# Longer slots for split activations: a distance in SBUF that differs from slot to slot

## The chip, the cores and the metric

The kernel runs on one core of a Trainium2 chip. The metric is the device time of one execution in microseconds. Engines are named as in the profile: PE is TensorE, PEld its loading of weights, DVE VectorE, ACT ScalarE, SP SyncE.

## The reference

A decoder trunk of two layers on one sequence of 256 tokens with 2048 features. The first layer is recurrent, the second attends within a window and has attention sinks; each is followed by a SwiGLU feed-forward block of width 5632, and one pair of keys and values is projected between them.

```python
for layer in range(DEPTH):                       # DEPTH = 2
    if layer < N_REC:                            # N_REC = 1
        x = recurrent_block(x, norm1_g[layer], lru_w_in[i], ...)   # 2048 -> 2 x 2048, gates 8 x 256 x 256, out 2048 -> 2048
    else:
        if layer == N_REC:
            k_band, v_band = shared_kv(x, kv_norm_g, w_kv, k_norm_g)   # 2048 -> 2 x 256
        x = attn_block(x, norm1_g[layer], w_q[j], ...)                 # 2048 -> 2048, window 128, out 2048 -> 2048
    x = swiglu_ffn(x, norm2_g[layer], ffn_w_in[layer], ffn_w_out[layer])   # 2048 -> 2 x 5632 -> 2048
```

All of it is float32.

## The kernel before

Activations lie with features on the 128 partitions and the 256 tokens along the free dimension. Each float32 operand of a big product is split into two float32r parts, a high part (the rounded value) and a low part (what the rounding left), and a product is the sum of three matmuls: high weights by high activations, high weights by low activations, and low weights by high activations.

The weights come from HBM in tiles of 128 x 1024 (512 KB), one per *job*. A job is two tiles of the contraction (`k` = 0, 1) by four tiles of 128 output features (`f` = 0 to 3), so 24 matmuls of 128 x 128 weights and 256 columns. `load` (L241) brings a tile into one of four buffers `raw`; `split` writes its high part to one of four buffers `hi` on ACT (L259) and its low part to one of four `lo` on DVE (L260). `stream` goes through the jobs in order: it loads four jobs ahead, splits three jobs ahead, and runs the job's matmuls.

The activations lie in *slots*, 58 of them, which `slot` hands out and `free` takes back in a queue. A slot has 2 x 256 float32 on each partition: the high part in its first half (1024 bytes), the low part in the second. `split_act` fills it (ACT by L113, DVE by L122). Slots also serve as plain float32 scratch. A job needs two slots, `x2[0]` and `x2[1]`, one for each `k`.

`products` writes the matmuls of a job: the weights are a slice of 128 columns (512 bytes) of `hi` or `lo`, and the moving operand is the high half ("a"), the low half ("b") or, in a few places, the whole slot ("h", 512 columns in one matmul) of `x2[k]`:

```python
w = (hi if high else lo)[:, k * 512 + f * P:k * 512 + f * P + P]
args = (ps[f][0][:, 0:c1 - c0], w, x2[k][:, c0:c1])
```

They are at L323, and at L321 where another matmul was put ahead of one. In most jobs the order alternates between `k` = 0 and 1 after two to four matmuls; in the last job of a group it does after three. The gates of the recurrent block have their own matmuls (L641) with slots moving, 24 for each of eight jobs. The projection of keys and values (eight jobs) does twelve matmuls with slots moving (L832) and then twelve with the slots as weights and `hi` or `lo` moving (L841 to L843). Norms, attention scores, transposes and the like are plain float32 matmuls through `pe_other` (L331, L334). `warm` (L268) runs 15 matmuls on zeros at the start.

The buffers are placed one after another in SBUF, in the order in which they are made: parameters, constants, `x`, `raw`, `hi`, `lo`, scratch, and then the slots. On each partition `hi` begins at byte 54752 and each of `hi` and `lo` is 4096 bytes long, so all eight begin at 480 modulo 512. `s0` begins at byte 104992, which is 32 modulo 512, and a slot is 2048 bytes.

Of the kernel before, what the change touches and what calls it, by code (L numbers as in the profile page):

```python
# [17 lines left out]
P = 128  # L18
D = 2048
T = 256  # L20
# [28 lines left out]
class Trunk:  # L49
# [12 lines left out]
    WARM = 15  # L62
    SYNC = (0, 2, 5)
    RUNS = 3
    DVE_TICK = 640.0
    ACT_TICK = 800.0

# [71 lines left out]

    def slot(self, dt=F32R):  # L140
        i = self.slots.popleft()
        s = self.spool.tile([P, 2 * T], dt, tag=f"s{i}", name=f"s{i}")
        self.held[id(s)] = (i, s)
        return s

# [54 lines left out]
    def run_bg(self):  # L200
        self.dve = min(max(self.dve - self.DVE_TICK, -self.SPARE), self.DEBT)
        self.act = min(max(self.act - self.ACT_TICK, -self.SPARE), self.DEBT)
        while self.dve < self.DVE_TICK and self.act < self.ACT_TICK:
            task = next((t for t in self.bg if t[0] <= self.tick), None)
            if task is None:
                break
            self._step(task)
# [81 lines left out]
    def products(self, todo, st, hi, lo, x2, last, keep=False, paired=False):  # L289
# [7 lines left out]
        while rest:  # L297
# [3 lines left out]
            if self.other is not None:  # L301
                self.runs = self.RUNS
            if not keep and self.runs and rest[0][2] != "h":
# [436 lines left out]
    def kv(self, xs, r, gains):  # L740
# [65 lines left out]
        for c in range(8):  # L806
            def mm(hi, lo, c=c):
                if c == 0:
                    st["ps"] = [self.bank() for _ in range(4)]
                    self.DVE_TICK, self.ACT_TICK, self.SPARE = self.LATER  # L810

# [319 lines left out]
```

## Time and profile before

| | |
|---|---|
| median of three runs | 1990.26 us (1989.77 to 1990.41) |
| span of the profiled execution | 1988.6 us |
| its time beside the median | the span is 1.7 us below the median of the runs; no other time of that execution was taken |
| PE busy | 1982.0 us, 16684 matmul records |
| DVE, ACT busy | 1271.2 us, 1067.9 us |
| HBM read | 371.88 MB, 188 GB/s over the span |

A matmul's duration in the profile reaches from its start to the modelled end of its pipeline, and the next one starts before that. How fast matmuls follow one another is read from their starts: from the timeline, from the chain in order of time, or from a count in a stretch.

### The profile page before, as it was taken

The numbers are of one execution on the slowest core, as the hardware profiler recorded it, in microseconds if no ns is written. First come the engines' busy times: TensorE is split into PE (matmuls) and PEld (weight loads), VectorE is DVE, ScalarE is ACT, GpSimd is POOL, SyncE is SP. The second block draws the span as 40 slices with busy tenths as digits, with TensorE's granted clock in tenths as the row PEclk, the third lists the DMA queues.
The fourth block names the chain that finished last, engine by engine and source line by source line (L and its number), as shares of the span: only waits on it lengthen the run. The fifth ranks groups of instructions, "written<-read, shape, count | busy, mean of one in ns | idle before, by whom it ended". The sixth has DMA issues, their size and how long they took to land.

```text
span 1988.6 us, 40066 instructions
## 1 busy us (share of the span) xinstructions
PE 1982.0 (100%) x16684; PEld 1935.5 (97%) x16684; DVE 1271.2 (64%) x2049; ACT 1067.9 (54%) x1624; POOL 0.2 (0%) x4
## 2 busy tenths in 40 slices
PE   9999999999999999999999999999999999999999
PEld 9999999999999999999999889999999999999999
DVE  8988876556556655545668786755565565554453
ACT  7798655444444444444556775544454454444442
POOL 0000000000000000000000000000000000000000
PEclk9999999999999999999999999999999999999999
DMA  8555655565556555556555435565566656656663
GB/s 279 185 187 182 211 191 192 196 196 191 192 195 196 191 192 196 195 191 194 197 186 167 134 101 163 188 197 195 191 193 196 195 191 194 197 193 203 204 208 128
DMA packets 105302, 376.58 MB, mean 189 GB/s; under 512 B 11808, under 2 KB 14240, under 8 KB 105120
## 3 DMA queue, kind: packets, MB, share of 16 engines
q1 hardware_dynamic: 104832, 373.88, 57.8%
q8 instruction: 130, 2.13, 0.4%
q14 instruction: 52, 0.43, 0.1%
q10 hardware_dynamic: 288, 0.14, 0.0%
HBM read 371.88 MB, written 2.10 MB: 188 GB/s over the span
## 4 chain that ended last, share of the span: by engine, by line
PE 99%; ACT 0%; DVE 0%; DMA 0%; issue 0%; ACTq 0%
PE b L323 94%; PE b L334 2%; PE b L641 1%; PE b L331 1%; PE b L832 1%; ACT s L113 0%; PE b L321 0%; PE b L841 0%; PE b L842 0%; PE b L843 0%; DMA x<-in_x 0%; DVE s L131 0%; DVE lo L260 0%; ACT L113 0%; DVE s L122 0%
## 5 line engine op out<-in xcount | busy, mean ns | idle before, releaser
L323 PE MATMUL b<-s,hi 128*128 128x256 f32 (+1 forms) x10276 | 1431.9, 285 | 0.4 <-ACT s L113 0.4
L323 PEld LDWEIGHTS b<-s,hi 128*128 128x128 f32 x10276 | 1313.4, 188 | 30.4 <-ACT s L113 0.7
L260 DVE TENSOR_TENSOR lo<-raw,hi 128x1024 fp32r<-128x1024 f32 (+1 forms) x705 | 861.4, 1223 | 651.2 <-ACT hi L259 648.1
L259 ACT ACTIVATE hi<-raw 128x1024 fp32r<-128x1024 f32 (+1 forms) x705 | 745.7, 1059 | 817.7 <-PE b L323 756.7
L323 PE MATMUL b<-s,lo 128*128 128x256 f32 x5504 | 831.8, 277 | 0.0
L323 PEld LDWEIGHTS b<-s,lo 128*128 128x128 f32 x5504 | 720.4, 188 | 2.4 <-issue 0.8
L113 ACT ACTIVATE s<-h 128x256 fp32r<-128x256 f32 (+1 forms) x106 | 40.8, 411 | 23.8 <-DVE h L122 23.8
L113 ACT ACTIVATE t<-b 128x256 f32<-128x256 f32 x136 | 49.8, 374 | 2.5 <-PE b L323 0.3
L113 ACT ACTIVATE s<-x,par 128x256 fp32r<-128x256 f32 x80 | 38.6, 499 | 19.3 <-DVE x L122 13.6
L113 ACT ACTIVATE s<-s 128x256 f32<-128x256 f32 (+1 forms) x112 | 39.6, 409 | 5.7 <-DVE s L126 5.5
L113 ACT ACTIVATE h<-h 128x256 f32<-128x256 f32 (+1 forms) x104 | 38.8, 375 | 2.1
L113 ACT ACT_TABLE_LOAD x30 | 38.5, 1283 | 0.5
L126 DVE SCALAR_TENSOR_TENSOR s<-x,par,s 128x256 fp32r<-128x256 f32 x80 | 37.5, 482 | 1.4 <-ACT s L113 0.8
L122 DVE TENSOR_TENSOR h<-b,rstd 128x256 f32<-128x256 f32 x100 | 37.6, 417 | 0.0
L122 DVE TENSOR_TENSOR x<-x,b 128x256 f32<-128x256 f32 x64 | 24.1, 418 | 21.0 <-PE b L323 21.0
L113 ACT ACTIVATE s<-s,h 128x128 f32<-128x128 f32 x64 | 28.3, 443 | 13.3 <-DVE h L131 13.2
L122 DVE TENSOR_TENSOR h<-h,rstd 128x256 f32<-128x256 f32 x94 | 35.4, 419 | 0.0
L122 DVE TENSOR_TENSOR h<-h,h 128x256 f32<-128x256 f32 x88 | 35.0, 420 | 0.4 <-ACT h L113 0.4
L122 DVE TENSOR_TENSOR s<-h,s 128x256 fp32r<-128x256 f32 x88 | 35.2, 420 | 0.1
L122 DVE TENSOR_TENSOR h<-b,t 128x256 f32<-128x256 f32 x92 | 34.6, 417 | 0.0
L122 DVE TENSOR_TENSOR s<-s,s 128x256 fp32r<-128x256 f32 (+1 forms) x80 | 30.9, 422 | 3.5 <-ACT s L113 3.5
L334 PE MATMUL b<-s,s 64*128 64x256 f32 (+3 forms) x292 | 29.0, 302 | 0.1
(99 smaller groups left out, 566.4 us busy)
## 6 DMA issues: line engine op xcount, KB each, us to landing
raw<-in_ffn_in SPq DMA_DIRECT2D x352, 512.0 KB, 3.5
raw<-in_ffn_out SPq DMA_DIRECT2D x176, 512.0 KB, 4.3
raw<-in_lru_in SPq DMA_DIRECT2D x63, 512.0 KB, 3.6
raw<-in_lru_out SPq DMA_DIRECT2D x32, 512.0 KB, 3.7
raw<-in_w_q SPq DMA_DIRECT2D x32, 512.0 KB, 3.3
raw<-in_w_o SPq DMA_DIRECT2D x32, 512.0 KB, 3.3
raw<-in_gate SPq DMA_DIRECT2D x8, 512.0 KB, 3.9
raw<-in_kv SPq DMA_DIRECT2D x8, 512.0 KB, 4.3
```

Source lines behind the costliest of these rows:

```text
L113: self.nc.scalar.activation(out, in_, func, **kw)
L122: self.nc.vector.tensor_tensor(out, a, b, op)
L126: self.nc.vector.scalar_tensor_tensor(out, a, s, b, op0, op1)
L259: self.nc.scalar.activation(hi[:, q], raw[:, q], AF.Copy)
L260: self.nc.vector.tensor_tensor(lo[:, q], raw[:, q], hi[:, q].bitcast(F32), ALU.subtract)
L323: self.nc.tensor.matmul(*args, **kw)
L331: self.other = self.ins(f(*args, **kw))
L334: self.other = self.ins(f(*args, **kw))
L641: nc.tensor.matmul(out[j], (hi if high else lo)[:, c:c + P], x2[kt][:, q:q + T], start=kt == 0 and high > q, stop=kt == 1 and not high)
L832: nc.tensor.matmul(ps[f][:, 0:T], w0, x2[kt][:, q:q + T], start=k0 + kt == 0 and high > q, stop=k0 + kt == ND - 1 and not high)
```

## The change

Each slot's tile gets 8 more float32 (32 bytes) on each partition, and the slot that is handed out is its first 512 elements. Nothing else differs: the line numbers behind it grow by 1 or 2, so L323 becomes L325.

```diff
     RUNS = 3
+    STEP = 8
...
     def slot(self, dt=F32R):
         i = self.slots.popleft()
-        s = self.spool.tile([P, 2 * T], dt, tag=f"s{i}", name=f"s{i}")
+        w = self.spool.tile([P, 2 * T + self.STEP], dt, tag=f"s{i}", name=f"s{i}")
+        s = w[:, 0:2 * T]
         self.held[id(s)] = (i, s)
```

Slot `i` then begins 2080 bytes, not 2048, after the one before it.

## The prediction

> **What bounds the kernel now.** I read the page first: the busy times, the row of the granted clock and the chain that ended last, then the costliest groups.
>
> ```profile
> span 1988.6 us, 40066 instructions
> ...
> PE 1982.0 (100%) x16684; PEld 1935.5 (97%) x16684; DVE 1271.2 (64%) x2049; ACT 1067.9 (54%) x1624; POOL 0.2 (0%) x4
> ...
> PEclk9999999999999999999999999999999999999999
> ...
> PE 99%; ACT 0%; DVE 0%; DMA 0%; issue 0%; ACTq 0%
> PE b L323 94%; PE b L334 2%; PE b L641 1%; PE b L331 1%; PE b L832 1%; ACT s L113 0%; PE b L321 0%; PE b L841 0%; PE b L842 0%; PE b L843 0%; DMA x<-in_x 0%; DVE s L131 0%; DVE lo L260 0%; ACT L113 0%; DVE s L122 0%
> ...
> L323 PE MATMUL b<-s,hi 128*128 128x256 f32 (+1 forms) x10276 | 1431.9, 285 | 0.4 <-ACT s L113 0.4
> L323 PEld LDWEIGHTS b<-s,hi 128*128 128x128 f32 x10276 | 1313.4, 188 | 30.4 <-ACT s L113 0.7
> ```
>
> PE is busy all the span, the clock is granted in full, and 99% of the chain is matmuls on PE that wait for nothing else. So the time is the number of matmuls times the distance in time from one start to the next, which I call the spacing. Only what changes the spacing can move the end. The mean of a matmul (285 ns) is no spacing, since matmuls are pipelined. The load of weights (188 ns) is longer than the spacing too, so the load for the next matmul runs beneath the present one, and the two read SBUF at once: that is what the change touches.
>
> The spacing comes from the chain in order of time, whose pieces give a start, a length and a count of matmuls.
>
> ```profile
> 74.19 2.72 PE b L641 x24
> 76.91 21.76 PE b L323 x192
> ...
> 123.14 5.44 PE b L641 x48
> ...
> 155.81 22.78 PE b L323 x192
> 178.59 5.65 PE b L641 x48
> ```
>
> Here stands the fact on which I build. The same 192 matmuls of the same line take 21.76 us in one piece (113.3 ns each) and 22.78 us in another (118.6 each). The 48 of L641 take 5.44 us (113.3) or 5.65 (117.7). The spacing has two states, about 4.4 ns (4%) apart, in the same kernel, with the clock full. I call them the short and the long state. The piece at 155.81 may hold some waits besides, so I take the smaller step, the 4.4 of L641.
>
> The long stage of feed-forward matmuls is all in the short state. The groups of the stretch from 400 to 1000 us, with shapes kept apart, show it:
>
> ```profile
> L323 PE MATMUL b<-s,hi 128*128 128x256 f32 x3149 | 418.8, 276 | 0.0
> L323 PE MATMUL b<-s,lo 128*128 128x256 f32 x1766 | 263.6, 276 | 0.0
> L323 PE MATMUL b<-s,hi 128*128 128x512 f32 x189 | 53.5, 392 | 0.0
> ```
>
> Counting a 512-column matmul as two units of 256 columns there are 3149 + 1766 + 2 x 189 = 5293 units in 600 us: 113.4 ns. The third row says one thing more. It has one load of weights (188 ns, above) for 512 columns, and its second 256 columns cost 392 - 276 = 116 ns, no less than a unit with a load beneath it. So the 113.3 seem to be the price of streaming 256 columns, and not of a meeting of the two reads.
>
> Elsewhere the long state holds for long. In the stretch from 1171 to 1230 us the groups have a longer mean for the same shape:
>
> ```profile
> L323 PE MATMUL b<-s,hi 128*128 128x256 f32 x220 | 31.3, 282 | 0.0
> L323 PE MATMUL b<-s,lo 128*128 128x256 f32 x120 | 19.0, 280 | 0.0
> ```
>
> **The change, part by part.** It removes and adds no instruction, and in the built programs the order on every engine and every wait are the same. Only addresses move. Before, slot i begins at 104992 + 2048 i bytes, so every slot is 32 modulo 512; the buffers hi and lo begin at 480 modulo 512, and all slices of weights are whole steps of 512 bytes. The distance from weights to moving operand is 64 modulo 512 for every one of the matmuls of L321, L323, L641 and L832. After, a slot is 2080 bytes and the distance is 64 + 32 i modulo 512: sixteen distances, each for three or four of the 58 slots. Counting in the built order, the distance changes at 5000 of 16,193 places, once in 3.2 matmuls.
>
> The groups of the whole run, with shapes kept apart, say how much work that is:
>
> ```profile
> L323 PE MATMUL b<-s,hi 128*128 128x256 f32 x9570 | 1291.3, 277 | 0.4 <-ACT s L113 0.4
> L323 PE MATMUL b<-s,lo 128*128 128x256 f32 x5504 | 831.8, 277 | 0.0
> L323 PE MATMUL b<-s,hi 128*128 128x512 f32 x706 | 201.6, 393 | 0.0
> ...
> L321 PE MATMUL b<-s,hi 128*128 128x512 f32 x13 | 6.6, 510 | 0.0
> ```
>
> That is 9570 + 5504 + 2 x 706 + 2 x 13 = 16,512 units; eight jobs of gates and eight of keys and values, with 24 each, make 16,896.
>
> What other distances cost is shown in one place only, the projection of keys and values. There L832 has slots as moving operand and hi or lo as weights (distance 64), and after each twelve, L841 to L843 have it the other way round (slots as weights, hi or lo moving: distance -64, which is 448); at each turn one matmul runs over a load at distance 0. From the timeline (start, length, engine and line):
>
> ```profile
> 1013.80 0.39 PE L832 MATMUL b<-s,hi 128*128 128x256 f32 x2
> ...
> 1015.16 0.28 PE L841 MATMUL b<-hi,s 128*128 128x256 f32 x1
> ...
> 1016.46 0.28 PE L843 MATMUL b<-hi,s 128*128 128x256 f32 x1
> 1016.58 0.40 PE L832 MATMUL b<-s,hi 128*128 128x256 f32 x2
> 1016.82 0.28 PE L832 MATMUL b<-s,lo 128*128 128x256 f32 x1
> ...
> 1018.00 0.28 PE L841 MATMUL b<-hi,s 128*128 128x256 f32 x1
> ...
> 1019.37 0.39 PE L832 MATMUL b<-s,hi 128*128 128x256 f32 x2
> ```
>
> Twelve of L832 take 1015.16 - 1013.80 = 1.36 us (113.3 ns): short state. At the very matmul where the distance changes the state becomes long: 1016.58 - 1015.16 = 1.42 us (118.3). Back at 64 it stays long (1018.00 - 1016.58 = 1.42), and at the next turn to 448 it falls back to short (1019.37 - 1018.00 = 1.37). No wait and no other work marks the first turn. So the state isn't fixed by the distance, since both occur at 64 and at 448, but a change of distance can throw it over, and it then lasts. The 48 matmuls average (1019.37 - 1013.80) / 48 = 116.0 ns.
>
> This is the nearest row to a kernel whose distance keeps changing, so I take 116.0 as its spacing. Now it is 113.4, and some 130 us of the span (25 us from 156, half of the projection of keys and values, most of 1160 to 1230, some shorter pieces, an estimate by the views above) are at 4.4 more: about 1100 units, 0.3 ns in the mean, so 113.7. The difference is 2.3 ns x 16,896 = 39 us.
>
> To this comes the turn itself. The three starts from 1016.46 to 1016.82 are 360 ns apart, against 3 x 117.7 = 353: some 6 ns for a turn. The turns from 1018.00 on show about 2 or less. With 5000 turns that is between 0 and 30 us, of which 16,896 / 12 x 6 = 8 us at most are in the 116.0 already. A step of 32 is smaller than the 384 here, so I take 6 us. The sum is 1988.6 + 39 + 6 = 2033.6 for the span, and with the 1.7 us between the span and the median of 1990.26 it is 2035 us.
>
> The bounds of this cost: below, every matmul at the short spacing, 0.3 x 16,896 = 5 us less than now, 1985; above, every matmul in the long state, (117.7 - 113.7) x 16,896 = 68 us, and all turns at 6 ns, 22 us more: 2080.
>
> The rest is covered. ScalarE and VectorE write and read the slots at new addresses, but DVE has 36% of the span idle and ACT 46%; even 5% on all DVE work (64 us) would lie beside PE. If that cover were gone, PE would wait for slots, and the idle columns of L323 (0.4 and 0.0 us now) would show it. The transfers go to raw, which doesn't move. The few fp32 matmuls of L331 and L334 read two slots or a slot and a constant; at 3% of the chain (L334 2%, L331 1%: 60 us) even a 4% change is 2 us.
>
> **The rivals.** First: *no change*. If the state hangs on when a matmul starts and not on the addresses, the kernel stays at 1990, 1985 to 1994. For it speaks that both states occur at distance 64. The Trainium skill, "SBUF — State Buffer", section "SBUF: two separate sides", says that PE has two independent read ports, one for the moving operand and one for the weights, and that PE never waits on anyone there; by this rule the change moves nothing and the time is 1990. The trace disagrees in part: the spacing went from 113.3 to 118.3 at the matmul where the operands change places. Also on this side lies the case in which mixed distances end each long stretch early: at best 5 us, 1985.
>
> Second: *faster*. If the 113.3 themselves come from how the slots lie (all of them are 32 modulo 64 now, half of them would be 0 modulo 64), then some distances are below it. No row shows a shorter spacing, so I bound the gain by the only step that rows show, 4.4 ns, for half of the units: 2.2 x 16,896 = 37 us, 1953; for a quarter, 1971. Against it stands the 512-column row: its second half has no load beneath it and costs the same. The Trainium skill, "TensorE: Matmul & The Clock Gate", section "Wait — 56ns, not 53.3ns?", gives N / 2.4 GHz + 2.5 ns at full clock, 109.2 ns for 256 columns. By that figure there would be 4.1 ns to win on each unit; here 113.3 is measured, and no run tells yet why.
>
> Third: *much slower*. If some of the sixteen distances hold the long state or worse whatever came before, and each turn costs its 6 ns, the time goes to the upper bound, 2058 to 2080, and past it if a distance exists that costs more than 118. Nothing in the trace shows more than 118 for long.
>
> That the change doesn't do what it says is ruled out by the addresses in the built program.
>
> **How the numbers follow.** A measurement of this kernel tells some 0.2% (4 us) from no change. A mixture of the two states, 1995 to 2058: 0.54. The upper case, 2058 and more: 0.12. No change: 0.12, of which 0.02 are below 1986. Faster by a lower spacing: 0.22. So faster 0.24, same 0.10, slower 0.66. The forecast is that of the likeliest case, 2035. The range leaves out about one in ten on each side: down to 1968, just past a quarter of the units at the shorter spacing, and up to 2078; alone, the likeliest case would have 1995 to 2058.
>
> **What would show it.** Right: in the profile after, the clock stays full, idle times stay near zero, and the chain's pieces of 192 matmuls of L323 (by its new line number) at 77 us take about 22.3 us instead of 21.76; in the stretch from 400 to 1000 us the mean of a 256-column matmul rises from 276 to about 279, and fewer units fit in it, some 5170 instead of 5293. The projection of keys and values, which alternates already, changes least. Wrong: the mean there falls below 276 (then slot placement was the price), stays at 276 (then the distance doesn't matter), or PE shows idle time before matmuls, named by a releaser.

## The result and the profile after

The changed kernel takes 2060.0 us (2059.58 to 2060.41), the kernel before 1990.3 us: a ratio of 1.0349, interval 1.0335 to 1.0364. It is slower and inside the range; it moved by 69.7 us, half as much again as the 45 that were forecast. The profiled execution spans 2058.2 us, 69.6 us more than before.

The page after, in the rows that answer to those of before:

```profile
span 2058.2 us, 40066 instructions
...
PE 2051.6 (100%) x16684; PEld 2003.9 (97%) x16684; DVE 1272.4 (62%) x2049; ACT 1068.0 (52%) x1624; POOL 0.2 (0%) x4
...
PEclk9999999999999999999999999999999999999999
...
PE 99%; ACT 0%; DVE 0%; DMA 0%; issue 0%; ACTq 0%
...
L325 PE MATMUL b<-s,hi 128*128 128x256 f32 (+1 forms) x10276 | 1477.6, 289 | 0.5 <-ACT s L114 0.5
...
L325 PE MATMUL b<-s,lo 128*128 128x256 f32 x5504 | 856.1, 281 | 0.0
```

The clock is full, PE has the same 16684 records and no more idle time (0.5 us before L325, 0.4 before), and DVE and ACT are busy as long as before (1272.4 and 1068.0 us). The same matmuls simply follow one another more slowly. In the chain in order of time (start, length, line, count) the pieces of equal work in the recurrent block show by how much:

```profile
76.20 2.83 PE b L643 x24
79.03 22.71 PE b L325 x192
...
127.33 5.68 PE b L643 x48
...
161.33 22.76 PE b L325 x192
184.09 5.68 PE b L643 x48
```

192 matmuls took 21.76 us before, and take 22.71 (118.3 ns each). The second 192, which before ran in the long state (22.78), are unchanged at 22.76. The 48 of the gates are all at 5.68, where before some were at 5.44 and some at 5.65. So the short state is nearly gone. The stretch from 400 to 1000 us, groups with shapes kept apart:

```profile
L325 PE MATMUL b<-s,hi 128*128 128x256 f32 x3000 | 416.1, 281 | 0.0
L325 PE MATMUL b<-s,lo 128*128 128x256 f32 x1696 | 262.5, 281 | 0.0
L325 PE MATMUL b<-s,hi 128*128 128x512 f32 x192 | 55.0, 395 | 0.0
```

3000 + 1696 + 2 x 192 = 5080 units in 600 us are 118.1 ns, against 113.4. Worked out from the starts of all 256-column matmuls that follow another without a gap, the mean spacing is 113.6 ns before and 118.1 after; 4.5 ns for some 15,450 of them is 69.5 us, about the whole difference.

### The profile page after: what moved, and what is told of

The parts are those of the page before. It is cut to its first block, busy times and chain, and to the rows that moved or that the text cites. A ratio compares the mean times of both kernels' runs of the same rounds, so it can differ in the third digit from the quotient of the medians.

```text
span 2058.2 us, 40066 instructions
## 1 busy us (share of the span) xinstructions
PE 2051.6 (100%) x16684; PEld 2003.9 (97%) x16684; DVE 1272.4 (62%) x2049; ACT 1068.0 (52%) x1624; POOL 0.2 (0%) x4
## 4 chain that ended last, share of the span: by engine, by line
PE 99%; ACT 0%; DVE 0%; DMA 0%; issue 0%; ACTq 0%
PE b L325 94%; PE b L336 2%; PE b L643 1%; PE b L333 1%; PE b L834 1%; ACT s L114 0%; PE b L323 0%; PE b L843 0%; PE b L845 0%; PE b L844 0%; DMA x<-in_x 0%; DVE s L132 0%; ACT L114 0%; DVE lo L262 0%; DVE s L902 0%
## 5 line engine op out<-in xcount | busy, mean ns | idle before, releaser
L325 PE MATMUL b<-s,hi 128*128 128x256 f32 (+1 forms) x10276 | 1477.6, 289 | 0.5 <-ACT s L114 0.5
L325 PEld LDWEIGHTS b<-s,hi 128*128 128x128 f32 x10276 | 1350.2, 188 | 32.0 <-ACT s L114 0.8
L325 PE MATMUL b<-s,lo 128*128 128x256 f32 x5504 | 856.1, 281 | 0.0
L325 PEld LDWEIGHTS b<-s,lo 128*128 128x128 f32 x5504 | 740.2, 188 | 2.3 <-issue 0.8
```

What stands on the lines that cost most here:

```text
L325: self.nc.tensor.matmul(*args, **kw)
```

## The experiments

Two theories stood against each other. *Change*, which the forecast used: both states occur at any distance, and it is the changing that throws the matmuls into the long one. *Set*: the spacing belongs to the distance, and most of the sixteen are worse than 64. All runs but the last two leave the slots as they were before the change or move them as a whole; in every kernel the matmuls and their order are those of before. Distances are the moving operand's address less that of the weights loaded beneath it, which are the next matmul's. The runs `a_blocks`, `b_perjob`, `c_align`, `h_sixteen` and `d_fine` were timed once each; eight runs of the kernel before, timed beside the later ones, lay between 1989.7 and 1991.3 us.

**Sixteen distances, each held for 45 jobs (a_blocks).** High and low weights of a buffer lie in one tile with room to shift them:

```diff
-        self.hi = [const.tile([P, 1024], F32R, name=f"hi{i}") for i in range(4)]
-        self.lo = [const.tile([P, 1024], F32R, name=f"lo{i}") for i in range(4)]
+        self.wts = [const.tile([P, 2048 + 128], F32R, name=f"hi{i}") for i in range(4)]
...
+    def parts(self, i):
+        o = 8 * (i // 45 % 16)
+        w = self.wts[i % 4]
+        return w[:, o:o + 1024], w[:, o + 1024:o + 2048]
```

> The slots keep one residue; instead the weights' buffers move: job i puts its high and low weights 32 x (i // 45 mod 16) bytes further on, so that each of the sixteen distances is held for 45 jobs (about 1060 matmuls, 120 us) and then changes once. Theory 'change': both states occur at any distance, and it is the changing that throws the matmuls into the long one. Then nearly all blocks run at the 113.4 ns of before, but for a long stretch here and there: 1990 to 2005 us. Theory 'set': the spacing belongs to the distance, 64 is one of the good ones, and most of the others cost 116 to 119 ns however long they are held. Then the blocks differ from each other, each is steady within, and the sum comes near the changed kernel: 2040 to 2065 us.

Measured: 2058.0 us, nearly the 2060.0 of the changed kernel, with 73 changes of distance, where that has 5041 (counted over all float32r matmuls in the built order; the 5000 of the prediction are those of the jobs alone). The theory *change* falls. Seven stretches of 100 us, each within one block (L327 is L323 of before; the count in brackets is what to read), and one of before with the same kind of job:

```profile
270.00:370.00 100.00, 99.37 (x788) 1.00 0.56 184
400.00:500.00 100.00, 100.00 (x809) 1.00 0.56 187
530.00:630.00 100.00, 100.00 (x813) 1.00 0.57 186
655.00:755.00 100.00, 100.00 (x816) 1.00 0.58 189
...
1345.00:1445.00 100.00, 100.00 (x800) 1.00 0.56 184
1470.00:1570.00 100.00, 100.00 (x809) 1.00 0.56 185
1600.00:1700.00 100.00, 100.00 (x810) 1.00 0.57 189
```

```profile
530.00:630.00 100.00, 100.00 (x842) 1.00 0.60 195
```

These are the distances 0, 480, 448, 416 and, later, 256, 224 and 192: all have fewer matmuls than the 842 of before. Such counts also depend on the jobs in the stretch (the first holds more 512-column matmuls than the others, and a short break), so the distances are compared by the starts. The mean spacing in ns of each block, by the distance modulo 256 (two blocks each), is alike for what lies 256 apart:

```
distance    0      32     64     96     128    160    192    224
first     119.8  117.4  113.5  120.0  118.7  117.4  117.8  118.4
second    119.8  117.1  115.0  120.0  118.9  117.4  117.8  118.4
```

Cut into six parts, most blocks agree within 0.3 ns from part to part. (The second block at 64 is broken by other stages: it holds 204 matmuls at 113.3 besides, and the 115.0 of the rest is a mixture of the two states.) In this run the short state is seen at 64 modulo 256 alone. Weighting these with the shares in which the changed kernel uses its distances (and, for 64, the 117.7 of its long state) gives 118.4 ns, against 118.1 measured there.

**A new distance with each job (b_perjob).** The same kernel with `o = 8 * (i % 16)`.

> As the run with blocks, but the weights move by 32 bytes with each job (i mod 16), so all sixteen distances occur, each for one job of 24 matmuls at a time, and none changes within a job. Theory 'change': a change every 24 matmuls is half as often as in the projection of keys and values (116.0 ns with one in 12), so 114.5 to 116 ns, 2005 to 2030 us. Theory 'set': as with the blocks, 2040 to 2065 us, since the same distances have the same weight.

Measured: 2063.6 us, again as *set* has it. Yet one thing differs from the blocks: the matmuls at 64 and 320, reached from another distance each time, take 117.4 and 117.6 ns, not 113.5. History does count, at that distance.

**Address or distance (c_align).** One gap of 32 bytes ahead of `hi`:

```diff
+        self.gap = const.tile([P, 8], F32, name="gap")
         self.hi = [const.tile([P, 1024], F32R, name=f"hi{i}") for i in range(4)]
```

> A gap of 32 bytes ahead of the weights' buffers moves weights and slots alike: the distance stays 64 everywhere, but both lie at 0 modulo 64 (weights 0, slots 64 modulo 512) instead of 32. Theories 'change' and 'set' alike: the distance is the same, 1988 to 1992 us. Theory 'alignment': the absolute address counts, half of the changed kernel's slots differ from before in it, and the time moves by more than 10 us either way.

Measured: 1990.5 us beside 1989.8 before, and the same piece of 192 matmuls at 21.76 us:

```profile
77.16 21.76 PE b L324 x192
```

With this one shift, of 32 bytes, the absolute address doesn't count where the distance stays. The "faster" rival of the prediction, which hung on it, goes.

**A change between distances that are alike (e_256).** `o = 64 * (i % 2)`, so 64 and 320 in turn.

> The weights of every second job lie 256 bytes further on, so the distance is 64 and 320 in turn and changes with each job of 24 matmuls. In the run with blocks, distances 256 apart had the same spacing (0 and 256 119.8 ns, 192 and 448 117.8, 64 and 320 113.4 to 115). Theory 'set, period 256': nothing is lost by changing between two that are alike, 1988 to 1998 us. Theory 'change': the run with a new distance in each job gave 2063.6 us; if its changes were the cost, this one has as many and comes to 2030 us or more.

Measured: 1989.9 us, a ratio of 0.9999 (0.9988 to 1.0011). The distance changes 748 times and nothing is lost. From 400 to 1000 us the groups make 4915 + 2 x 189 = 5293 units, as many as before:

```profile
L327 PE MATMUL b<-s,hi 128*128 128x256 f32 x4915 | 567.4, 276 | 0.0
L327 PE MATMUL b<-s,hi 128*128 128x512 f32 x189 | 53.5, 391 | 0.0
```

So the period is 256, and a change between two distances that are alike is free.

**One bad distance, never changed (g_const96).** The gap of 32 bytes stands ahead of the slots.

> A gap of 32 bytes ahead of the slots: the distance is 96 everywhere and never changes. Theory 'set': the block at 96 ran at 120.0 ns against 113.65 of before, so 6.3 ns x 16,896 units = 107 us more: 2085 to 2100 us, slower than the changed kernel. Theory 'change': without a change of distance the short state holds, 1990 to 2000 us.

Measured: 2089.0 us, 1.0498 (1.0453 to 1.0543): slower than the changed kernel, without any variation. The stretch from 400 to 1000 us has 2963 + 1673 + 2 x 189 = 5014 units, 119.7 ns:

```profile
L324 PE MATMUL b<-s,hi 128*128 128x256 f32 x2963 | 415.5, 282 | 0.0
L324 PE MATMUL b<-s,lo 128*128 128x256 f32 x1673 | 261.1, 282 | 0.0
L324 PE MATMUL b<-s,hi 128*128 128x512 f32 x189 | 54.3, 395 | 0.0
```

This kernel also shows where the cost lies. From the starts, its 256-column matmuls are 6.3 ns further apart than before (120.0 against 113.6), but its 512-column ones only 4.2 ns (233.5 against 229.3). With twice the columns the surcharge doesn't double: it is a cost per matmul, and each matmul has one load of weights beneath it. That the two reads get in each other's way is the reading that fits; the runs don't show the memory itself.

**How fine the good point is (h_sixteen and d_fine).** Blocks again, with steps of 16 bytes (`o = 4 * (i // 45 % 16)`) and of 4 bytes (`o = 57 + i // 45 % 16`).

> Blocks of 45 jobs again, with distances 16 bytes apart, 64 down to 336 modulo 512, which modulo 256 is each sixteenth once. If the spacing goes by lines of 32 bytes, each odd sixteenth copies its neighbour (48 like 32, or 80 like 64) and the sum stays near the 2058 us of the blocks; if it goes by smaller lines, the new eight differ from both neighbours, and one of them may be as short as 64 (113.4 ns).

> Blocks of 45 jobs with distances 4 bytes apart, from 348 down to 288 modulo 512 (92 to 32 modulo 256), so around the 64 of before. Theory 'lines of 32 bytes': 64 to 92 all run like 64 (113.4 ns) and 32 to 60 like 32 (117.3): 2020 to 2030 us. Theory 'a single good point': all but 64 lie between 117 and 120 ns, 2050 to 2070 us. If some block runs below 113.3 ns, the short state of before is not a floor.

Measured: 2061.6 and 2055.6 us. Most of the new steps differ from the step 16 bytes below them (48: 116.7, 80: 118.1, 144: 119.9 ns, where 32, 64 and 128 take 117.2, 113.5 and 118.7), so lines of 32 bytes are not the rule. In steps of 4 bytes 60 takes 118.0 in the mean, 64 takes 113.3 and 68 takes 118.3: around 64 a single good point. Stretches of the second kernel, in the blocks at 76, 72, 68 and 64 modulo 256, and one of before that has the same kind of job as the last two:

```profile
530.00:630.00 100.00, 100.00 (x813) 1.00 0.57 187
655.00:755.00 100.00, 100.00 (x813) 1.00 0.57 189
780.00:880.00 100.00, 100.00 (x824) 1.00 0.56 186
910.00:1010.00 100.00, 100.00 (x867) 1.00 0.58 194
```

```profile
780.00:880.00 100.00, 100.00 (x869) 1.00 0.60 194
```

No block of any kernel runs below 113.3 ns: that stays the floor. Two blocks show the short state elsewhere too: 192 modulo 256 ran 204 matmuls at 113.4 ns and elsewhere mostly at 117.8, and 88 began at 120.0, ran at 113.3 from 148 to 190 us, and then mostly at 120.0 again. Other distances have two paces above the floor: 208 ran at 123.3 ns until 926 us and at 117.8 from there, and one of the blocks at 128 began at 120.0 and went on at 118.7. So a distance doesn't fix one pace.

**Slots that differ by 256 bytes (s_256).** The change itself, with a step that should do no harm:

```diff
-        s = self.spool.tile([P, 2 * T], dt, tag=f"s{i}", name=f"s{i}")
+        w = self.spool.tile([P, 2 * T + (64 if i % 6 == 5 else 0)], dt, tag=f"s{i}", name=f"s{i}")
+        s = w[:, 0:2 * T]
```

> The changed kernel with a harmless step: every sixth slot is 256 bytes longer instead of each 32, so the slots lie at distances 64 and 320 in groups of six. The distance then differs from slot to slot, and in the built order it changes at 1803 places, many of them within a job. Theory 'set, period 256': the two are alike, nothing is lost: 1987 to 1997 us. Theory 'change', in the form in which a change within a job costs: 1803 places against 5041 of the changed kernel, a third of its 70 us and more, 2010 us or above.

Measured: 1990.4 us, a ratio of 1.0001 (0.9989 to 1.0012). Its units from 400 to 1000 us are 3151 + 1764 + 2 x 189 = 5293, the very number of before:

```profile
L324 PE MATMUL b<-s,hi 128*128 128x256 f32 x3151 | 418.9, 276 | 0.0
L324 PE MATMUL b<-s,lo 128*128 128x256 f32 x1764 | 263.2, 276 | 0.0
L324 PE MATMUL b<-s,hi 128*128 128x512 f32 x189 | 53.5, 391 | 0.0
```

**Two distances, one of them good (k_two).** The same line with `(8 if i == 28 else 0)`.

> One gap of 32 bytes behind slot 28: the first 29 slots stay at distance 64 (9173 matmuls), the others lie at 96 (6899), and the two are mixed in 2059 places. Theory 'set' alone: the matmuls at 64 keep 113.65 ns and those at 96 take 120.0: 6899 / 16,072 x 16,896 x 6.3 ns = 46 us, 2036 us. Theory 'set and history': a matmul at 64 that comes behind one at 96 is thrown into the long state and stays there, so most of those at 64 take 117.5 instead: up to 37 us more, 2055 to 2075 us. The spacing of the matmuls at 64 alone tells the two apart.

Measured: 2056.9 us, 1.0335 (1.0305 to 1.0365), where *set* alone gave 2036. From the starts, the matmuls at 96 take 119.6 ns, and those at 64 take 116.8 in place of 113.6; thirty matmuls and more after the last one at 96 they still average 115.9. The groups from 400 to 1000 us give 3018 + 1704 + 2 x 192 = 5106 units, 117.5 ns:

```profile
L324 PE MATMUL b<-s,hi 128*128 128x256 f32 x3018 | 416.7, 280 | 0.0
L324 PE MATMUL b<-s,lo 128*128 128x256 f32 x1704 | 262.1, 280 | 0.0
L324 PE MATMUL b<-s,hi 128*128 128x512 f32 x192 | 54.9, 394 | 0.0
```

So it is *set and history*: of the distances tried, 64 modulo 256 is the one at which the short state lasts through whole blocks, and a matmul at another distance throws those behind it out of it, often for long.

What ends the long state is to be seen in the trace of before. Row by row (start, length, engine and line), the fence shows eight matmuls in 0.94 us ahead of a run of three 512-column matmuls (the third row, with two of 256 columns behind them), and eight in 0.90 us after it, at one distance and without a wait:

```profile
228.84 1.10 PE L323 MATMUL b<-s,hi 128*128 128x256 f32 x8
229.78 0.63 PE L323 MATMUL b<-s,lo 128*128 128x256 f32 x4
230.25 1.09 PE L323 MATMUL b<-s,hi 128*128 128x512 f32 x5
231.18 0.62 PE L323 MATMUL b<-s,lo 128*128 128x256 f32 x4
231.63 1.07 PE L323 MATMUL b<-s,hi 128*128 128x256 f32 x8
232.53 0.73 PE L323 MATMUL b<-s,lo 128*128 128x256 f32 x5
```

Outside the projection of keys and values, the long state of before begins at the start of the kernel or where the stream of these matmuls is broken (two starts some 90 ns or more further apart than usual, or a matmul of another kind between). In 16 of 17 cases it ends at such a run; 16 of the 30 such runs that came in the long state ended it, and none of the 189 in the short state did. The changes of pace at 88, 128 and 208 stand at such runs as well. In `k_two`, matmuls at 64 that come behind one at 96 average 117.4 ns as long as no such run has passed, and 115.8 after one. No run here takes the 512-column matmuls out, so this is seen and not tested.

## Why the prediction was right, and where it was not

*The bound.* Right. PE is never short of work before or after, and the 69.6 us are spacing alone. DVE and ACT, with new addresses for their slots, are busy as long as before; the idle time of L325 is 0.5 us.

*Two states, and a floor at 113.3.* Right as far as it went. None of the 28 distances tried (modulo 256) runs below it, and the reason that was given (the second half of a 512-column matmul costs no less) agrees with the surcharge of the bad distance, which doesn't grow with the columns.

*"The state isn't fixed by the distance ... but a change of distance can throw it over."* Half right, and the step that was mis-sized. At 64 it holds: in `k_two` and `b_perjob` the short state is lost after another distance. But a change between distances that are alike costs nothing (`e_256`, `s_256`), and a distance that is never changed can cost 5% (`g_const96`). The prediction read the turns in the projection of keys and values as turns of a state that all distances share. They were turns between 64 and 448, and 448 is 192 modulo 256, a distance that has both states too; in the blocks at the other twelve of the sixteen only longer spacings were seen.

*The term 116.0 ns.* That row was a half-and-half mixture of the two states, at two distances. The changed kernel has 118.1. In its parts: 84.5% of its matmuls stand at distances other than 64 and 320 and average 118.3 ns, which makes 4.0 of the 4.5 ns; the 15.5% at 64 and 320 average 117.0, which makes the other 0.5. So the term of 39 us should have been near 69.

*The term for turns, 6 us.* Too large, if anything. Matmuls at a place where the distance changes are 0.3 ns longer in the changed kernel than the others (118.35 against 118.03), 1.5 us in all.

*The rivals.* The upper case, "some of the sixteen distances hold the long state or worse whatever came before", with 2058 to 2080, is the one that came, and it had a chance of only 0.12; the likeliest case, with its 1995 to 2058, was missed by 2 us. That 2060 lies inside the range is luck in part, since the range was that wide for the sake of the rivals. The upper case's price held for another reason than its sum: the distances go up to 120 ns, past the 118 that the trace of before showed, while the turns cost almost nothing. The case of no change is out: `g_const96` moves nothing but the slots, by 32 bytes, and loses 99 us. The Trainium skill ("SBUF — State Buffer", section "SBUF: two separate sides") says that PE never waits on anyone there; the 1990 us that the prediction drew from this didn't come. For the faster case, `c_align` shows that moving both to 0 modulo 64 gains nothing. The 109.2 ns for 256 columns, an estimate by the formula of the Trainium skill ("TensorE: Matmul & The Clock Gate", section "Wait — 56ns, not 53.3ns?"), are reached by these float32r matmuls at none of the distances tried; 113.3 is the least measured.

*The signs.* A piece of 192 matmuls was to take 22.3 us and took 22.71; the mean was to be 279 and is 281; 5170 units were forecast and 5080 fit. The projection of keys and values changed less than the rest, as was said. In the chain, twelve of L834 start each job:

```profile
1057.80 1.42 PE b L834 x12
...
1060.64 1.42 PE b L834 x12
```

A job of 24 takes 2.84 us there, 118.3 ns against the 116.0 of before: 2.3 more, where all matmuls together have 4.5.

Left open: what in the memory makes 64 modulo 256 the good point, why the floor is 113.3, and why a break in the stream or a run of three 512-column matmuls can switch the state. The stretch that before spent in the long state at 64 around 1171 to 1230 us begins at such a break, at 1158.5 us, and ends at such a run, at 1227.7.

## What to carry to other kernels

When PE is the bound and its matmuls follow without a gap, read the spacing from starts or counts and not from durations: here 3.5% of the time hung on the bytes between the moving operand and the next matmul's weights, and an innocent pad of 32 bytes ahead of a pool cost 5%. Whoever adds, pads or reorders buffers in such a kernel should keep that distance (or keep it modulo 256) and look at the count of matmuls in a fixed stretch before and after. And a row that shows a cost at two values of a thing doesn't price the other fourteen: a sweep in blocks within one run does.

## What the runs showed of the hardware that was not expected

- The spacing of 256-column float32r matmuls depends on the distance between moving operand and weights, to 4 bytes, with a period of 256 bytes: 113.3 ns at 64, and 116.7 to 120.7 in the mean of most blocks at the others, with 123.3 for a while at 208. The clock was granted in full in every profile that has its row (all but that of `h_sixteen`).
- It didn't depend on where the two lie in the one shift that was tried: 32 bytes more for both leaves 1990.5 us.
- At some distances there are two lasting states (64: 113.3 and 117.7 ns, 192: 113.4 and 117.8, 88: 113.3 and 120.0). Matmuls at other distances and breaks in the stream bring the longer one at 64, and 16 of 17 times a run of three 512-column matmuls ended it.
- The surcharge doesn't grow with the columns: 6.3 ns for 256 columns and 4.2 for 512 at distance 96.
